# A hybrid encoder layer on one core: small operations sorted and dealt out in the values' stage, and four reorderings around the first loads, the latents and the rotary products

## The chip, the cores and the metric

The kernel runs on one core of one Trainium2 chip. The metric is the time of one execution in device microseconds. The core's engines are TensorE (PE in the profile, with its weight loads as PEld), VectorE (DVE), ScalarE (ACT), GpSimd (POOL) and SyncE (SP, which issues nearly all transfers here). Each works through its own queue of instructions in order and waits on semaphores for the others.

## The reference

One layer with 1024 tokens and 16 meta tokens put in front, model width 1024, all in float32:

```python
def _mixer(u, ...):
    proj = u @ w_in                       # u = rmsnorm(h)
    rq, rk, rv, rg, a_cq, a_ckv, a_kr, a_gret, a_gmla = jnp.split(proj, SPLIT_IDX, axis=-1)
    rq, rk = rope(rq), rope(rk) * RET_DK ** -0.5
    y_ret = head_group_norm(bidir_retention(rq, rk, rv, decay_f, decay_b))
    y_ret = (jax.nn.silu(rg) * y_ret) @ w_ret_out
    q = rmsnorm(a_cq) @ w_uq              # its rotary part is rotated
    k_nope, v = rmsnorm(a_ckv) @ w_uk, rmsnorm(a_ckv) @ w_uv
    k_rope = rope(a_kr)                   # one for all heads
    y_mla = softmax_attention(q, k_nope, k_rope, v) @ w_mla_out
    merged = jax.nn.sigmoid(a_gret) * y_ret + jax.nn.sigmoid(a_gmla) * y_mla
    return merged @ w_o
```

Behind it follow a residual add, an RMSNorm, a SwiGLU feed-forward block, another residual add and a last RMSNorm. The retention needs tables of exponentials of its 16 decay rates (8 heads, two directions).

## The kernel before

**Products.** A float32 operand is split into a rounded high part (a cast on ScalarE) and the rest (a subtraction on VectorE); a product is three matmuls, high by high, high by low, low by high. The helper `split` (line 155) does this for the weights, `bsplit` (278) and `bscale` (284, 285) for the tokens; `split.done` holds the last two instructions. Large products go by Winograd's form of Strassen's scheme: `seven` (lines 184 to 230) loads the four quarters of a weight block (190), forms sums of them (192 to 194, and 210 for the last), splits each of seven operands when it is asked for (212, 213), and issues 12 matmuls of 128 x 512 for each (220). The sums are on GpSimd. The seven partial products are called 11, t2, t3, n1, 21, t4 and 22; `seven_out` (236 to 245) adds them up. Tokens need the same seven combinations, kept in `U`.

**Stages of the first 680 us.** (1) First products: 11 and 21 of seven weight blocks as the tokens arrive, one weight block at a time (`wfirst` splits at 155, products at 344), then the rest of the first two blocks with `rest_out` (305 to 317). The combinations t3 and t4 of the tokens are formed in between, four operations each (412 and 417), with their splits (414, 278, 279). The meta tokens' tile `um` is cleared on GpSimd (406). (2) Two more blocks, the squares of the tokens, and sums of the value weights (545 to 554, GpSimd) that go through device memory. (3) Values: `project_values`, seven products of four steps q each; each step loads a weight (562), splits it and issues twelve matmuls (568), and two for the meta tokens (571) where they belong to the product. Between the products, `between[n]` holds other work: `input_norm` and `decays` behind the second, `decay_rows` (16 exponentials, 513) and a third of the 19 unfinished gates behind the fourth, `decay_columns` and another third behind the fifth, the rest behind the sixth. A gate is loaded, multiplied on VectorE (530), put through silu or sigmoid on ScalarE (531) and stored. `unfinished` lists 16 silus and then 3 sigmoids, and the thirds are taken with a stride of 3. (4) Four rotary blocks of the retention, `project_rope`. (5) The retention of eight heads with blocks of gates and latents as fillers for TensorE. (6) Latents: `project_q`, `project_key`, `project_kv` and the last gate block; `latent_part` (794 to 802) scales, splits and squares a tile and adds the square to `lss`; `latent_norm` sums `lss` over channels with matmuls by ones (161) and makes a norm factor on VectorE and ScalarE. What is left for the meta tokens is put off into `pending` and done within the next block: for the key, a transpose (887), `shared_key` (825 to 832, small operations on 48 x 16 with tables loaded for it), then the norm. (7) The retention's output, four blocks by `seven` (`ret_out`), with the queries' rotary tiles `xx` (`gemm`, lines 139 to 141) made ahead of the third block and rotated (`rotary`, 977 to 984) as that block's results come.

**What sets the order.** The code gives a priority by its order; a planner places every instruction ahead of the run by a simulated clock, first what is ready and earliest in the code, on each engine's queue. `tc.issue_after(ins)` holds the instructions of a block behind `ins` on the same engine. Tiles come from pools; a tile is given out when the one before it in its place is no longer used, and a load into it waits for that.

## Time and profile before

| | |
|---|---|
| median of 3 runs | 1756.33 us (1754.27 to 1756.72) |
| profiled execution | 1753.05 us |
| its span, first to last instruction | 1751.1 us |
| granted TensorE clock, mean | 0.991 |
| TensorE busy | 1698.3 us |
| VectorE busy | 1346.8 us |
| ScalarE busy | 852.2 us |
| GpSimd busy | 763.6 us |

The profile is one execution. The windows view gives, for a stretch in microseconds from the span's start, the busy time and the number of instructions of each engine, the granted TensorE clock (1.00 is full), the mean busy share of the 16 DMA engines and what they moved. The timeline gives instructions in order: start, duration, engine, line, operation, output and inputs, count; in square brackets stands the time in which the engine had been idle before and what ended it. The view by lines gives a group's busy time and the mean of one in ns, and after the bar the idle time before them. A matmul's duration is longer than its distance to the next, since they overlap.

### The profile page before, as it was taken

The page shows a single profiled execution, that of the slowest core. Times are in us where ns is not written, and L with a number is a line of the kernel's source. Part 1 is how long each engine was busy: PE and PEld are TensorE (multiplying, and loading weights), DVE is VectorE, ACT ScalarE, POOL GpSimd, SP SyncE. Part 2 cuts the span into 40 slices and gives each one's busy share as a digit, 9 for nine tenths or more (in the row PEclk, how much of TensorE's full clock was granted, in tenths as well). Part 3 has the DMA queues.
Part 4 walks back from the last instruction along what each step waited for, and adds up shares of the span by engine and source line. Part 5 has one row for each costly group of instructions (what it writes and reads, how often), then busy time and mean ns, then how long its engine had stood idle before and what let it go on. Part 6 is the DMA issues. An engine that isn't in the chain of part 4 may idle for free. (4 is left out here: it accounts for less than half of the span.)

```text
span 1751.1 us, 26268 instructions
## 1 busy us (share of the span) xinstructions
PE 1698.3 (97%) x8644; PEld 1427.5 (82%) x8644; DVE 1346.8 (77%) x2461; ACT 852.2 (49%) x1597; POOL 763.6 (44%) x585
## 2 busy tenths in 40 slices
PE   8999999999999999999999999999999999999998
PEld 6787677888887778999898888788888888788787
DVE  7846778888789876888888768776778887866775
ACT  7426566344424624778787346433333333522335
POOL 2450267575653421324322501566676666523431
PEclk9999999999999999999999999999999999999999
DMA  7876924566546875111122844233344445876612
GB/s 261 290 250 207 296 85 131 164 211 212 193 150 226 254 280 178 30 45 30 30 64 69 272 150 162 80 108 115 129 142 144 139 138 167 273 269 226 231 61 97
DMA packets 169913, 287.15 MB, mean 164 GB/s; under 512 B 20841, under 2 KB 46882, under 8 KB 169778
## 3 DMA queue, kind: packets, MB, share of 16 engines
q1 hardware_dynamic: 168626, 284.44, 48.8%
q8 instruction: 68, 1.11, 0.3%
q10 hardware_dynamic: 1152, 1.05, 0.2%
q14 instruction: 67, 0.55, 0.1%
HBM read 193.28 MB, written 92.06 MB: 163 GB/s over the span
## 5 line engine op out<-in xcount | busy, mean ns | idle before, releaser
L220 PE MATMUL mm<-slot,slot 128*128 128x512 f32 x2604 | 595.0, 390 | 3.6 <-DVE slot L213 1.9
L220 PEld LDWEIGHTS mm<-slot,slot 128*128 128x128 f32 x2604 | 487.3, 188 | 110.2 <-DVE slot L213 4.1
L212 ACT CAST slot<-slot 128x512 fp32r<-128x512 f32 (+1 forms) x385 | 226.8, 596 | 432.2 <-PE mm L220 339.5
L213 DVE TENSOR_TENSOR slot<-slot,slot 128x512 fp32r<-128x512 f32 (+1 forms) x385 | 350.2, 912 | 67.8 <-ACT slot L212 66.9
L192 POOL TENSOR_TENSOR slot<-slot,slot 128x512 f32<-128x512 f32 (+1 forms) x57 | 78.7, 1381 | 329.5 <-DMA slot<-in_w_in 116.5
L220 PE MATMUL mm<-ht,slot 128*128 128x512 f32 x552 | 184.2, 397 | 1.9 <-DVE slot L213 1.9
L220 PE MATMUL mm<-h,slot 128*128 128x512 f32 x440 | 153.2, 408 | 5.8 <-ACT slot L212 2.8
L210 POOL TENSOR_TENSOR slot<-slot,slot 128x512 f32<-128x512 f32 (+1 forms) x57 | 76.5, 1343 | 140.8 <-DVE slot L213 97.6
L155 DVE TENSOR_TENSOR slot<-slot,slot 128x512 fp32r<-128x512 f32 x123 | 97.1, 806 | 40.4 <-ACT slot L155 36.2
L220 PEld LDWEIGHTS mm<-ht,slot 128*128 128x128 f32 x552 | 103.1, 188 | 23.8 <-DVE slot L213 2.7
L155 ACT CAST slot<-slot 128x512 fp32r<-128x512 f32 x123 | 74.5, 618 | 76.7 <-POOL slot L1275 23.4
L1092 DVE TENSOR_SCALAR_CACHE_REDUCE pr<-s,sq_c 128x384 f32<-128x384 f32 (+1 forms) x192 | 103.3, 572 | 7.9 <-PE t L1110 5.3
L220 PE MATMUL mm<-lt,slot 128*128 128x512 f32 x276 | 108.6, 394 | 0.0
L220 PEld LDWEIGHTS mm<-h,slot 128*128 128x128 f32 x440 | 84.2, 193 | 26.3 <-ACT slot L212 5.3
L140 PE MATMUL mm<-slot,slot 128*128 128x512 f32 (+1 forms) x288 | 105.4, 366 | 0.0
L141 PE MATMUL mm<-slot,slot 128*128 128x512 f32 (+1 forms) x288 | 105.3, 366 | 0.0
L139 PE MATMUL mm<-slot,slot 128*128 128x512 f32 (+1 forms) x288 | 105.2, 367 | 0.0
L193 POOL TENSOR_TENSOR slot<-slot,slot 128x512 f32<-128x512 f32 (+1 forms) x57 | 83.4, 1463 | 48.6 <-DVE slot L213 42.3
L1105 DVE TENSOR_TENSOR ptl<-t,pth 128x512 fp32r<-128x512 f32 x128 | 85.7, 684 | 17.7 <-ACT pth L1104 17.2
L1136 POOL TENSOR_TENSOR oa<-oa,ob 64x256 f32<-64x256 f32 x32 | 24.0, 749 | 151.8 <-ACT ob L1135 151.8
L220 PE MATMUL mm<-l,slot 128*128 128x512 f32 x220 | 88.6, 404 | 0.0
L1104 ACT CAST pth<-t 128x512 fp32r<-128x512 f32 x128 | 71.8, 579 | 25.2 <-PE t L1102 24.8
(409 smaller groups left out, 3667.6 us busy)
## 6 DMA issues: line engine op xcount, KB each, us to landing
slot<-in_w_in SPq DMA_DIRECT2D x90, 256.0 KB
f_d<-slot SPq DMA_DIRECT2D x71, 256.0 KB
slot<-f_d SPq DMA_DIRECT2D x71, 256.0 KB
slot<-in_xT SPq DMA_DIRECT2D x48, 256.0 KB
slot<-z_d SPq DMA_DIRECT2D x44, 256.0 KB
slot<-in_w_g SPq DMA_DIRECT2D x44, 256.0 KB
slot<-in_w_u SPq DMA_DIRECT2D x44, 256.0 KB
fl_d<-slot SPq DMA_DIRECT2D x42, 256.0 KB
```

The source lines that it names most:

```text
L139: pe.matmul(ps, sh, mh, start=start, stop=False)
L140: pe.matmul(ps, sh, ml, start=False, stop=False)
L141: pe.matmul(ps, sl, mh, start=False, stop=stop)
L155: split.done = act.copy(hi, t), dve.tensor_sub(lo, t, f(hi))
L192: pool.tensor_add(s1, a21, a22)
L193: pool.tensor_sub(s2, s1, a11)
L210: pool.tensor_sub(s2, s2, a12)
L212: act.copy(hi, side[b])
L213: dve.tensor_sub(low, side[b], f(hi))
L220: pe.matmul(ps, sw[:, ks], sx, start=begins and q == qs[0] and i == 0, stop=q == nq - 1 and i == 2, skip_group_check=True)
L1092: dve.tensor_scalar(pr[:, c], ps[:, :n], sq_c[:, qb : qb + 1], None, ALU.mult, ALU.max, accum_out=mx[:, j : j + 1])
L1105: dve.tensor_sub(pt[1][d], tp, f(pt[0])[d])
```

## The change

There are four groups of edits; no product of the reference is dropped, and nothing is computed in another precision.

First loads and first products: the first token block is issued from ScalarE's queue; the first use of the exponential (with its table load) stands behind the first weight's load; the meta tiles are cleared on VectorE at the start, and 13 matmuls of 384 columns read one of them and write a bank that nobody reads. The first two blocks change places, their weight sums go from GpSimd to VectorE (`adds=dve`), and the token combinations t3 and t4 are made within `rest_out`, behind t2 of both blocks; t4 and 22 are held behind the last weight split.

Values' stage: the work between is listed by product and step (`order`), decays first, then the norm, tables of two heads a step, rows of two heads a step, columns, then one gate a step in nine steps; the other ten gates follow the four rotary blocks, 3, 3, 2 and 2. All of it is held behind the split of its place. Gates are taken in the list's order, silus first.

Latents: both transposes of the kv latents' meta part come before their `latent_part`; the query norm comes before the shared key's meta part, whose transpose is held behind the last of the norm's matmuls.

Rotary products of the queries: the second half of `xx` is made behind 11, t2 and t3 of the third output block, and held behind their last matmul.

```diff
+NIDLE = 13
...
-    act.activation(warm, warm, AF.Exp)
...
     def token_sums(ps, sq, lo, blocks):
...
-            pe.matmul(ps[:n, b : b + 1], sq[:, b * P - lo : b * P - lo + n], ones, start=True, stop=True)
+            norm_sums.append(pe.matmul(ps[:n, b : b + 1], sq[:, b * P - lo : b * P - lo + n], ones, start=True, stop=True))
...
-    def seven(pools, srcs, blocks, meta=None):
+    def seven(pools, srcs, blocks, meta=None, adds=None):
         wr, ws, wh_, wl_, pm_ = pools
+        adds = adds or pool
...
-        pool.tensor_add(s1, a21, a22)
-        pool.tensor_sub(s2, s1, a11)
-        pool.tensor_sub(a21, a21, a11)
+        adds.tensor_add(s1, a21, a22)
+        adds.tensor_sub(s2, s1, a11)
+        adds.tensor_sub(a21, a21, a11)
...
+        for t in (um, umd):
+            dve.memset(f(t), 0.0)
...
             for prod, e, post in group:
                 dve.tensor_add(e, prod("t2"), e)
+            for make in late:
+                make()
...
+            idle = mk(pc, (P, 512), "mm")
+            for i in range(NIDLE):
+                pe.matmul(idle[:, : KT * 48], um.rearrange("p a b -> p (a b)")[:, :P], um.rearrange("p a b -> p (a b)"),
+                          start=True, stop=True)
...
-                x11.append(xload(2 * i, 0))
-                wa11.append(wfirst(win(i)[0], wf if i == 3 else wh1, wf if i == 3 else wl1))
+                x11.append(xload(2 * i, 0, nc.scalar.dma_start if i == 0 else load))
+                raw = wraw(win(i)[0])
+                if i == 0:
+                    act.activation(warm, warm, AF.Exp)
+                wa11.append(split(raw, wf if i == 3 else wh1, wf if i == 3 else wl1))
...
-                pool.memset(f(dst), 0.0)
...
+            def make_t3():
+                with tc.issue_after(made[0].ins), tc.issue_after(made[1].ins):
+                    for q in range(4):
+                        dve.scalar_tensor_tensor(x12[q], x12[q], col(2 * q), x22[q], ALU.mult, ALU.subtract)
+                        U[q]["t3"] = bsplit("t3", x12[q])
+
+            def make_t4():
+                with tc.issue_after(split.done[0].ins), tc.issue_after(split.done[1].ins):
+                    for q in range(4):
+                        dve.scalar_tensor_tensor(x21[q], x21[q], col(2 * q + 1), x11[q], ALU.mult, ALU.subtract)
+                        U[q]["t4"] = bsplit("t4", x21[q])
+                    for q in range(4):
+                        U[q]["22"] = bsplit("22", x22[q])
+
+            rest_out([(seven((wb, wf, wh1, wl1, pc), win(1), U, adds=dve), es[1], rg_post(1)),
+                      (seven(w7, win(0), U, adds=dve), es[0], rg_post(0))], cr, (make_t3, make_t4))
...
-        project_values({1: [input_norm, decays], 3: [decay_rows, lambda: finish_gates(unfinished[0::3])],
-                        4: [decay_columns, lambda: finish_gates(unfinished[1::3])],
-                        5: [lambda: finish_gates(unfinished[2::3])]})
+        order = [("21", 2, decays), ("21", 3, input_norm)]
+        order += [("t2", q, lambda q=q: decay_tables((2 * q, 2 * q + 1))) for q in range(4)]
+        order += [("t3", q, lambda q=q: decay_rows((2 * q, 2 * q + 1))) for q in range(4)]
+        order += [("n1", 0, decay_columns)]
+        order += [(nm, q, lambda: finish(1)) for nm, qs in (("n1", (1, 2, 3)), ("t4", (0, 1, 2)), ("22", (0, 1, 2))) for q in qs]
+        project_values({(nm, q): [f for m, p, f in order if (m, p) == (nm, q)] for nm, q, _ in order})
         for j in range(2):
             project_rope(j, False)
+            with tc.issue_after(split.done[0].ins), tc.issue_after(split.done[1].ins):
+                finish(3 if j == 0 else 2)
             project_rope(j, True)
+            with tc.issue_after(split.done[0].ins), tc.issue_after(split.done[1].ins):
+                finish(3 if j == 0 else 2)
...
                     pe.transpose(pt[:, k * NM : k * NM + NM], t[:, k * P : k * P + P], ident[:NM, :NM])
+                for k in range(2):
                     latent_part(pt[:, k * NM : k * NM + NM], tail, ckv_d[k], column(C_KVN + k), k == 0)
...
                 t = meta_sum(ps, P, 48)
-                pt = mk(pc, (P, 512), "mm")
-                pe.transpose(pt[:48, :NM], t, ident[:NM, :NM])
+                latent_norm(sq_c, 3, 96.0**-0.5, range(NB))
+                with tc.issue_after(norm_sums[-1].ins):
+                    pt = mk(pc, (P, 512), "mm")
+                    pe.transpose(pt[:48, :NM], t, ident[:NM, :NM])
                 ks = work(NM)[:48, :NM]
                 act.copy(ks, pt[:48, :NM])
                 shared_key(ks, tail)
-                latent_norm(sq_c, 3, 96.0**-0.5, range(NB))
...
         for lo, n in RCH:
-            for i in range(2):
-                xx[lo, i] = mk(pc, (P, 512), "mm")
-                gemm(xx[lo, i], wx[i], cq, 3, lo, n)
+            with ExitStack() as behind:
+                if lo:
+                    for b in ("11", "t2", "t3"):
+                        third(b)
+                    behind.enter_context(tc.issue_after(split.mm.ins))
+                for i in range(2):
+                    xx[lo, i] = mk(pc, (P, 512), "mm")
+                    gemm(xx[lo, i], wx[i], cq, 3, lo, n)
```

More of the change, by code (lines that the diff above doesn't have):

```diff
@@ L97, in build @@
     load(cols, A["cols"])
+    warm = mk(cp, (P, 1), "warm")
+    pool.memset(warm, 0.0)
     rstd = mk(cp, (P, NB + 1), "rstd")
@@ L209, in prod @@
                 if b == "22":
-                    pool.tensor_sub(s2, s2, a12)
+                    adds.tensor_sub(s2, s2, a12)
                 hi, low = slot(wh_, F32R)[:, :n], slot(wl_, F32R)[:, :n]
-                act.copy(hi, side[b])
-                dve.tensor_sub(low, side[b], f(hi))
+                split.done = act.copy(hi, side[b]), dve.tensor_sub(low, side[b], f(hi))
                 w[b] = hi, low
@@ L219, in prod @@
                 for i, (sw, sx) in enumerate(((wh, xh), (wh, xl), (wl, xh))):
-                    pe.matmul(ps, sw[:, ks], sx, start=begins and q == qs[0] and i == 0,
-                              stop=q == nq - 1 and i == 2, skip_group_check=True)
+                    split.mm = pe.matmul(ps, sw[:, ks], sx, start=begins and q == qs[0] and i == 0,
+                                         stop=q == nq - 1 and i == 2, skip_group_check=True)
                 if meta and b in meta[1]:
@@ L301, in rg_post, with rest_out @@
             return post
-        def rest_out(group, pl):
+        def rest_out(group, pl, late=None):
+            late = late or ()
             for prod, e, post in group:
                 dve.tensor_add(e, prod("t2"), e)
+            for make in late:
+                make()
             vs = [slot(pl) for _ in group]
@@ L334, in col, with wraw, wfirst @@
                 return column(C_MIX + k)
-            def wfirst(src, ph, plo):
+            def wraw(src):
                 raw = slot(wr1)
                 load(raw, src)
-                return split(raw, ph, plo)
+                return raw
+            def wfirst(src, ph, plo):
+                return split(wraw(src), ph, plo)
             def products(ps, w, b, q, begins):
@@ L495, in decays, with decay_tables @@
             dve.tensor_scalar(dec, dec, -1.0, None, ALU.mult)
+            dts[:] = [slot(xl) for _ in range(2)]
+        def decay_tables(heads):
             ip, im = idx[:, 0:P], idx[:, P : 2 * P]
-            dts = [slot(xl) for _ in range(2)]
-            for h in range(H):
+            for h in heads:
                 lf, lb = dec[:, h : h + 1], dec[:, H + h : H + h + 1]
@@ L504, in decays, with decay_rows @@
                 store(t_d[h], t)
-        def decay_rows():
+        def decay_rows(heads):
             rowf, rowb = idx[:, 2 * P : 3 * P], idx[:, 3 * P : 4 * P]
-            tts = [slot(xl), slot(sr)]
-            for h in range(H):
+            if not tts:
+                tts[:] = slot(xl), slot(sr)
+            for h in heads:
                 hs = slice((h % 2) * 64, (h % 2) * 64 + 64)
@@ L554, in value_weights, with value_product @@
             store(wv_d[3, q], a12)
-        def value_product(nm, meta):
+        def value_product(nm, meta, between):
             banks = [mk(pm, (P, 512), "mm") for _ in range(4)]
@@ L563, in value_product @@
                 hi, lo = split(raw, wh1, wl1)
+                with tc.issue_after(split.done[0].ins), tc.issue_after(split.done[1].ins):
+                    for fn in between.get((nm, q), ()):
+                        fn()
                 xh, xl_ = U[q][nm]
@@ L583, in project_values @@
                 a, meta = (0, M1[nm][1]) if nm in M1 else (1, M2[nm][1]) if nm in M2 else (0, None)
-                banks, mps = value_product(nm, meta)
+                banks, mps = value_product(nm, meta, between)
                 if nm == "t3":
@@ L616, in project_values @@
                     msum[a] = x
-                if n in between:
-                    with tc.issue_after(split.done[0].ins), tc.issue_after(split.done[1].ins):
-                        for fn in between[n]:
-                            fn()
         def project_rope(j, key):
```

32 lines of the change are left out of this document (11 added, 21 removed).

## The prediction

> **What bounds the kernel now.** I read the page's busy shares first, then the busy time of each engine by stage (the windows view, with stages cut where the code changes), then TensorE's waits, then the timeline around each wait.
>
> ```profile
> span 1751.1 us, 26268 instructions
> PE 1698.3 (97%) x8644; PEld 1427.5 (82%) x8644; DVE 1346.8 (77%) x2461; ACT 852.2 (49%) x1597; POOL 763.6 (44%) x585
> ```
>
> TensorE (PE) is busy for 97% of the span, so only 52.8 us are to be had by closing its gaps, beside what it loses at a lower clock. Where they lie:
>
> ```profile
> core 0: us, PE busy (x) PEld busy (x) DVE busy (x) ACT busy (x) POOL busy (x), PEclk, DMA share, GB/s
> ```
> ```profile
> 5.69:52.16 46.47, 41.60 (x162) 32.68 (x163) 42.57 (x58) 33.78 (x59) 9.54 (x6) 0.96 0.72 249
> 52.16:140.00 87.84, 87.84 (x396) 71.82 (x395) 54.93 (x79) 30.86 (x56) 38.59 (x26) 1.00 0.82 276
> 140.00:235.00 95.00, 88.95 (x395) 69.18 (x394) 67.35 (x118) 63.89 (x114) 19.02 (x14) 1.00 0.71 231
> 235.00:300.00 65.00, 62.97 (x304) 49.19 (x303) 54.10 (x71) 44.31 (x74) 46.05 (x29) 1.00 0.29 93
> 300.00:524.00 224.00, 222.40 (x1258) 187.91 (x1257) 184.60 (x445) 82.00 (x143) 139.38 (x96) 1.00 0.57 190
> 524.00:604.00 80.00, 72.64 (x339) 56.85 (x339) 73.11 (x130) 45.00 (x84) 32.51 (x20) 0.91 0.72 230
> 604.00:680.00 76.00, 73.55 (x319) 59.76 (x317) 49.31 (x75) 19.62 (x34) 17.02 (x13) 0.98 0.76 267
> 680.00:1751.10 1071.10, 1048.34 (x5480) 900.08 (x5480) 820.28 (x1491) 530.03 (x1030) 459.99 (x369) 1.00 0.40 132
> ```
>
> Subtract PE busy from the length: the first products idle 4.9 us, the values' stage (140 to 235) 6.1, the rotary products of retention (235 to 300) 2.0, the latents (524 to 604) 7.4, the output product with its rotary part (604 to 680) 2.5. Between 52 and 140 nothing is idle, between 300 and 524 1.6 us. So the edits sit where the gaps are, and dense PE work lies between them: what one place wins is handed on to the next. The clock column matters too; it drops just where PE had waited:
>
> ```profile
> 48.00:52.00 4.00, 4.00 (x12) 3.05 (x12) 4.00 (x8) 1.10 (x2) 0.00 (x0) 0.57 0.75 225
> 552.00:556.00 4.00, 4.00 (x13) 3.42 (x14) 3.78 (x8) 1.72 (x4) 1.01 (x1) 0.50 0.39 138
> ```
> ```profile
> 645.00:649.00 4.00, 3.29 (x8) 2.62 (x9) 4.00 (x6) 1.73 (x4) 2.69 (x2) 0.57 0.78 282
> ```
>
> At a granted 0.57 four busy microseconds do the work of 2.3: 1.7 lost; at 0.50, 2.0; the third window, 3.29 busy, loses 1.4. A wait of two to four microseconds therefore costs its length and about two more.
>
> **The change, part by part.**
>
> *First loads.* The first token block is issued from ScalarE's queue, so the first weight block moves up one place on SP. Thirteen matmuls on a zeroed tile run ahead.
>
> ```profile
> 1.18 0.42 SPq L330 DMA_DIRECT2D slot<-in_xT  x1
> 1.65 0.42 SPq L338 DMA_DIRECT2D slot<-in_w_in  x1
> ```
> ```profile
> 5.69 0.80 PE L344 MATMUL mm<-h,slot 128*128 128x512 f32 x1 [5.69 <-ACT slot L155]
> ```
> ```profile
> 49.29 1.05 PE L344 MATMUL mm<-h,slot 128*128 128x512 f32 x2
> 50.15 0.63 PE L344 MATMUL mm<-l,slot 128*128 128x512 f32 x1
> ```
>
> The second issue moves from 1.65 to 1.18: 0.47 us earlier, and the first real matmul waits for that weight's cast. On ScalarE the exponential's table load now stands behind that issue; it runs while ScalarE waits for data anyway. The idle matmuls cost at a low clock 0.43 us per 512 columns (50.15 less 49.29, over two), so 0.32 for their 384: 13 make 4.2 us.
>
> ```profile
> 1.48 0.42 POOL L406 MEMSET um<- 128x384 f32 x1
> ```
>
> Their operand's memset ends at 1.90 on POOL behind a dozen others; on VectorE, which has nothing ahead of it, it can begin when SP does, near 0.8, so they begin at about 1.2 and at 1.9 at the latest. They end between 5.4 and 6.1, against a first real product possible at about 5.2: they may delay it by 0.2 to 0.9. In return the products behind them start at full clock: bounds 0 (arrival of data sets the pace anyway) to 2.0 (the row at 0.50 above). I take 1.5 for start and clock together, near the middle, since pairs of blocks still have to arrive one after another.
>
> The Trainium skill, "TensorE: Matmul & The Clock Gate", section "What's actually happening", speaks against this edit: the gate looks at a free-running window of about 3.4 us, so how many matmuls stay slow depends on where in the window they fall. By that rule the 13 can end before the gate opens, the term is 0 and the sum stands 1.5 us higher. The low stretch of 48 to 52 agrees with the length, not with the phase, which no row here shows.
>
> *First products.* These rows tell the whole stall:
>
> ```profile
> 35.14 2.72 DVE L412 SCALAR_TENSOR_TENSOR slot<-slot,cols,slot 128x512 f32<-128x512 f32 x4
> ```
> ```profile
> 40.80 5.81 DVE L417 SCALAR_TENSOR_TENSOR slot<-slot,cols,slot 128x512 f32<-128x512 f32 x4
> 46.53 0.68 DVE L155 TENSOR_TENSOR slot<-slot,slot 128x512 fp32r<-128x512 f32 x1
> ```
> ```profile
> 41.41 1.29 POOL L192 TENSOR_TENSOR slot<-slot,slot 128x512 f32<-128x512 f32 x1 [12.35 <-DMA slot<-in_w_in]
> ```
> ```profile
> 47.26 0.73 PE L344 MATMUL mm<-h,slot 128*128 128x512 f32 x2 [4.34 <-DVE slot L155]
> ```
>
> Two groups of four equal operations: 2.72 us with POOL idle, 5.81 while POOL forms weight sums. The weight split that PE needs (L155) stands behind the slow group. The change moves the t3 and t4 blocks behind the split of the second t2 weight, and takes the sums of these two products from POOL to VectorE. Removed: the 4.34 us and the 1.7 at low clock, 6.0. Added on VectorE: 8 sums of 0.68 each, 5.4 us, less the 3.1 us of slowing. VectorE is the next to be late: 42.57 busy of 46.47 here; behind 52 it has 33 us spare in 88. PE has t2 and n1 of both products, 48 matmuls at 87.84/396 = 0.22 us, 10.7 us, to cover t3's blocks (four times 0.68 twice, 5.4) and the four splits (2.7). That suffices, with about a microsecond lost: I take -5.0, bounds -6.0 and 0. The token tiles are freed some microseconds later, so squares and value weights are loaded later; PE needs none of those before 140.
>
> *Values' stage.*
>
> ```profile
> L531 ACT ACT_TABLE_LOAD x7 | 9.0, 1283 | 0.1
> ```
> ```profile
> L513 ACT ACTIVATE slot<-slot,dec 64x128 f32<-64x128 f32 x16 | 5.5, 392 | 0.1
> ```
> ```profile
> 162.79 0.50 PE L568 MATMUL mm<-slot,hn 128*128 128x512 f32 x1 [1.25 <-ACT slot L155]
> ```
> ```profile
> L530 DVE TENSOR_TENSOR slot<-slot,rstd_b 128x512 f32<-128x512 f32 x19 | 14.1, 757 | 7.3 <-DMA slot<-rg_d 5.6 <-DMA slot<-g_d 1.6
> ```
>
> All 16 row exponentials run in one lump of 5.5 us, and the cast that PE needs stands behind it (162.79). Now at most four follow each split, and the 19 gates come one by one, silus before sigmoids: two table loads instead of seven, 5 x 1.283 = 6.4 us less on ScalarE. ScalarE is not the bound (63.89 of 95); what counts is PE's 6.1 us. Some of these waits have other causes (VectorE's tails between products), so -4.0, bounds -6.1 and 0.
>
> Ten gates move on into the retention's rotary products, two or three behind the last split of each.
>
> ```profile
> 204.50 1.39 DVE L530 TENSOR_TENSOR slot<-slot,rstd_b 128x512 f32<-128x512 f32 x1
> ```
>
> A gate's multiplication takes 0.76 in the mean, 1.39 beside POOL, which is busy 46 of 65 us there. VectorE has 65 - 54.1 = 10.9 us spare; ten gates want 7.6 to 13.9. Three of them ahead of the next split are 2.3 to 4.2 us, and the last product of the block before covers 12 x 0.22 = 2.7. So 0 to 1.5 us at each of four places: +2.0, bounds 0 and +6.
>
> *Latents.*
>
> ```profile
> 545.89 1.17 DVE L826 TENSOR_TENSOR small<-small,small 48x16 f32<-48x16 f32 x1 [1.37 <-DMA small<-in_cM]
> ...
> 549.54 1.71 DVE L800 TENSOR_TENSOR lss<-lss,slot 128x512 f32<-128x512 f32 x1
> ```
> ```profile
> 551.30 1.87 PE L161 MATMUL mm<-ones,lss 128*128 128x1 f32 x8 [3.65 <-DVE lss L800]
> ...
> 575.32 0.23 PE L860 MATMUL mm<-ident,sums 16*128 16x16 f32 x1 [0.64 <-DVE small L802]
> ```
>
> VectorE takes the meta tokens' shared key first, waits there for its cosine table, does three tiny operations at 1.2 us, and only then the sum of squares (L800) that PE's token sums wait for. The change puts the norm first and pins the key's transpose behind the token sums: 3.65 and 2.0 of clock go, 5.6. But VectorE is busy 73.11 of 80, so PE arriving earlier meets it again near 575. VectorE itself wins the 1.37 of waiting and up to 3 us of the tiny operations: I take -4.5, bounds -5.6 and -1.4. Issuing the latent transposes together removes the 0.64, but PE's next operand is late too: -0.5, bounds -0.6 and 0.
>
> *Rotary products of the queries.*
>
> ```profile
> 638.79 0.69 DVE L977 TENSOR_TENSOR slot<-mm,slot 128x512 f32<-128x512 f32 x1 [1.25 <-DMA slot<-in_cM]
> ```
> ```profile
> 645.71 0.80 PE L220 MATMUL mm<-h,slot 128*128 128x512 f32 x1 [2.02 <-ACT slot L212]
> ```
>
> All four rotary tiles are now made before the third output product; their VectorE work waits for tables and piles up, and a weight cast waits behind it. Afterwards three of the seven partial products (36 matmuls, 8 us) come between the two halves, so the work of the first half has PE work beside it and the second follows later. Removed 2.02 and 1.4 of clock; I take -3.0, bounds -3.4 and 0.
>
> *Sum.* -1.5 - 5.0 - 4.0 + 2.0 - 4.5 - 0.5 - 3.0 = -16.5 us. The profiled execution took 1753.05 us (1.95 around its span), so 1736.6; the median of the runs shown, 1756.33, lies 3.3 above that execution, and with it the forecast is 1756.33 - 16.5 = 1739.8.
>
> **Rivals.**
>
> *VectorE takes over as the bound.* In the first products it is 92% busy and gets 2.3 us more; in the latents 91%. If t4 and 22, following t3, come late once, and the latents give back all but VectorE's own saving, the first term falls to -1 and the latents to -1.9, and the sum is about -9: 1747. For it: those shares. Against: 33 us of slack right behind the first place.
>
> *The order hardly changes.* The instructions' order is a planner's, and the edits mostly add lower bounds on it; a gap closed at one place may open at another, since the planner did not foresee L800 coming 4 us late. Then the gains and new stalls of 3.65 + 2.0 each cancel, three of them: about 1756. Against: the pins act exactly on the operations that were late.
>
> *The gates hurt the rotary products.* Suppose each batch's loads sit on SP behind a weight load that waits for a buffer:
>
> ```profile
> 117.31 16.48 SPq L562 DMA_DIRECT2D slot<-wv_d  x7
> ```
>
> 2.4 us per issue. VectorE then holds the next split for 4.2 + 2.4, less the 2.7 covered, and 2.0 of clock follow: 5.9 at each of four places, 23.6 instead of the +2.0: 1756.33 - 18.5 + 23.6 = 1761.4. It decides from 18.5/4 = 4.6 us a place. For it: POOL's load there. Against: a DMA share of 0.29, and loads that can be issued early into six buffers.
>
> **How the numbers follow.** About 0.2%, 3.5 us, can be told from no change. Forecast 0.62, VectorE's bound 0.21, order unchanged 0.08, gates 0.09. The first two are faster, 0.83; the third 0.08 the same; the last slower, 0.09. The forecast's own range, with the bounds of its terms partly adding up, is 1730 to 1747; the second rival is taken in and the other two are left out: 1729 to 1751.
>
> **What would show it.** Right: no wait of PE above 1.5 us before 60; clock at 1.00 from 48 to 52; two table loads for the gates; no wait on lss; no wait above 1 us in the third output product. Wrong: waits on the split of weights (L213) between 235 and 300, or in the first products behind t3; a low clock at 550 or 645. The forecast fails as a whole if PE's busy time stays and its idle time falls by less than 5 us.

## The result, and the profile after

| | before | changed | ratio, 95% interval |
|---|---|---|---|
| first chip: median, runs | 1755.30 us (4; 1752.98 to 1756.72) | 1735.49 us (4; 1735.41 to 1735.73) | 0.9892 [0.9878, 0.9905] |
| another chip, the same two kernels | 1756.98 us (11) | 1738.01 us (5; 1734.51 to 1740.04) | 0.9893 [0.9877, 0.9910] |
| profiled execution | 1753.05 us, span 1751.1 | 1735.57 us, span 1733.6 | |

The change makes the kernel 1.1% faster, 19 to 20 us; 16.5 were forecast. The profile after, its span and its busy shares:

```profile
span 1733.6 us, 26277 instructions
PE 1693.8 (98%) x8657; PEld 1425.9 (82%) x8657; DVE 1356.3 (78%) x2471; ACT 839.9 (48%) x1588; POOL 748.5 (43%) x575
```

PE's idle time (span less busy) falls from 52.8 to 39.8 us. The other engines do about what they did, VectorE 9.5 us more (among it the sums it took over). So this is a story of waits, and the waits are read place by place. To do so I count PE's products of 128x512 ("long products" from here on), of which both kernels have 5628 in the same order of stages, and subtract the start times of products with the same number:

| place (number of the last long product) | start after | start before | after less before | won in this stage | forecast |
|---|---|---|---|---|---|
| start and first weights (80) | 26.14 | 26.56 | -0.42 | -0.4 | -1.5 |
| first products, both split blocks (480) | 122.38 | 128.95 | -6.57 | -6.2 | -5.0 |
| values' stage (760) | 194.56 | 208.47 | -13.91 | -7.3 | -4.0 |
| retention's rotary products, start of its heads (1200) | 318.08 | 329.14 | -11.06 | +2.8 | +2.0 |
| heads (1800) | 525.26 | 536.45 | -11.19 | -0.1 | 0 |
| latents (2020) | 596.48 | 608.33 | -11.85 | -0.7 | -5.0 |
| second and third output product (2280) | 655.42 | 671.53 | -16.11 | -4.3 | -3.0 |
| fourth, attention (2360) | 942.99 | 961.57 | -18.58 | -2.5 | 0 |
| to the end | 1733.59 | 1751.10 | -17.51 | +1.1 | 0 |

Stretches of the changed kernel, in the same columns as before (length, busy time and count of PE, weight loads, VectorE, ScalarE, GpSimd; granted clock; DMA share; GB/s):

```profile
48.00:52.00 4.00, 4.00 (x19) 3.32 (x18) 4.00 (x8) 3.37 (x8) 0.00 (x0) 1.00 0.49 145
560.00:564.00 4.00, 1.86 (x5) 1.06 (x6) 3.79 (x9) 1.47 (x4) 2.14 (x1) 0.55 0.95 301
564.00:568.00 4.00, 4.00 (x12) 3.14 (x12) 3.88 (x11) 1.82 (x5) 1.66 (x1) 0.60 0.95 317
592.00:596.00 4.00, 4.00 (x13) 3.18 (x13) 3.91 (x7) 2.18 (x4) 1.02 (x1) 0.68 0.76 243
645.00:649.00 4.00, 4.00 (x19) 3.34 (x18) 3.50 (x6) 1.24 (x3) 0.00 (x0) 1.00 0.99 395
```

The low clock behind the first products and in the third output product is gone, GpSimd no longer works beside VectorE at 48, but in the latents the low clock has only moved, from 552 to 560 and 592 (a granted clock of 0.5 is called half clock below; the windows mix it with full clock at their edges). The timeline of PE there (start, us, line; in brackets the idle time before and what ended it):

```profile
551.32 0.72 PE L223 MATMUL mm<-hn,slot 128*128 128x512 f32 x2 [1.50 <-DVE slot L216]
558.76 1.05 PE L164 MATMUL mm<-ones,lss 128*128 128x1 f32 x8 [0.76 <-DVE lss L837]
561.60 0.79 PE L223 MATMUL mm<-h,slot 128*128 128x512 f32 x1 [1.79 <-ACT slot L216]
...
588.42 0.50 PE L223 MATMUL mm<-ht,slot 128*128 128x512 f32 x1 [1.08 <-ACT ht L283]
...
591.04 1.32 PE L223 MATMUL mm<-h,slot 128*128 128x512 f32 x2 [0.88 <-ACT h L283]
```

The 3.65 us on the key's sum of squares are gone, and PE was 17.4 us ahead at the 1880th product; by the 2020th 5.6 of them had been given back. Those on L283 are for the split of Z, the retention's result, 28 tiles that are loaded, cast and subtracted between 540 and 597.

What the clock took is read from the trace's clock records: PE's busy time at half clock, halved. It is 10.6 us before (from 48, 550, 577, 645 and 874 on) and 4.3 after (from 560 and 591 on). PE's idle time between the first and the last product falls from 40.9 to 32.3. So of the 17.5 us, 8.6 are waits, 6.3 clock, and some 2.5 what is left: products beside a wait take longer, as the values' stage shows below, and the start changed.

### The profile page after: what moved, and what is told of

Same layout as the page of the kernel before. It is cut to its first block, busy times and chain, and to the rows that moved or that the text cites. A ratio compares the mean times of both kernels' runs of the same rounds, so it can differ in the third digit from the quotient of the medians.

```text
span 1733.6 us, 26277 instructions
## 1 busy us (share of the span) xinstructions
PE 1693.8 (98%) x8657; PEld 1425.9 (82%) x8657; DVE 1356.3 (78%) x2471; ACT 839.9 (48%) x1588; POOL 748.5 (43%) x575
## 5 line engine op out<-in xcount | busy, mean ns | idle before, releaser
L216 DVE TENSOR_TENSOR slot<-slot,slot 128x512 fp32r<-128x512 f32 (+1 forms) x385 | 354.3, 924 | 64.3 <-ACT slot L216 63.5
L196 POOL TENSOR_TENSOR slot<-slot,slot 128x512 f32<-128x512 f32 (+1 forms) x55 | 72.9, 1326 | 325.7 <-DMA slot<-in_w_in 86.1
L214 POOL TENSOR_TENSOR slot<-slot,slot 128x512 f32<-128x512 f32 (+1 forms) x55 | 74.1, 1347 | 136.5 <-DVE slot L216 94.4
L156 DVE TENSOR_TENSOR slot<-slot,slot 128x512 fp32r<-128x512 f32 x123 | 101.2, 840 | 40.4 <-ACT slot L156 37.8
L156 ACT CAST slot<-slot 128x512 fp32r<-128x512 f32 x123 | 74.5, 620 | 83.2 <-POOL slot L1320 23.4
L197 POOL TENSOR_TENSOR slot<-slot,slot 128x512 f32<-128x512 f32 (+1 forms) x55 | 81.0, 1472 | 58.4 <-DVE slot L216 55.9
L142 PE MATMUL mm<-slot,slot 128*128 128x512 f32 (+1 forms) x288 | 105.3, 365 | 0.0
L140 PE MATMUL mm<-slot,slot 128*128 128x512 f32 (+1 forms) x288 | 105.2, 367 | 0.0
```

Of the source, the lines that this page charges most:

```text
L140: pe.matmul(ps, sh, mh, start=start, stop=False)
L142: pe.matmul(ps, sl, mh, start=False, stop=stop)
L156: split.done = act.copy(hi, t), dve.tensor_sub(lo, t, f(hi))
L196: adds.tensor_add(s1, a21, a22)
L197: adds.tensor_sub(s2, s1, a11)
L214: adds.tensor_sub(s2, s2, a12)
```

## The experiments

All are edits of the changed kernel, timed against the kernel before on the same chip. Ratios are to that kernel; the changed kernel's is 0.9892 and 0.9893, so a ratio 0.001 higher is 1.75 us more. Where a place is named, the number is the start of that long product less that in the first profile of the changed kernel. Profiles that share the changed start already lie up to 1.55 us apart at the 80th product, so what a stage costs is the difference of two such numbers, at its end and at its start.

**Without the idle products.** `NIDLE = 13` becomes `NIDLE = 0`.

> The changed kernel (1735.5 us) without the 13 idle products ahead of the first real one; all else as changed. Theory (gains are local, and the start of the changed kernel gained only 0.4 us by its 80th long product): the time is 1735.9, up to 1736.5. Rival (the prediction's term: 1.5 us for the clock at the start): 1737.0. A third (the clock window at 48 to 52 belongs to the start as well): 1737.5 or more. What tells: the time of the 80th and of the 160th product of 128x512, beside the changed kernel's.

1739.04 us, ratio 0.9904 [0.9889, 0.9919]: 2 us more by the ratio. Yet the 80th product comes 0.34 us *earlier* than in the first profile, the 1200th 0.14 earlier, the 2340th 0.1 later. Clock is 1.00 from 48 to 52. Idle PE time in all is the same (32.1 against 32.3); what differs is half clock, 7.3 us against 4.3: from 296, 538, 562 and 859 on. Three of these stand behind waits that the changed kernel has as well (1.62 us for 1.18 at 294, and the same two at 561 and 857), one behind a wait of 1.56 at 537 that it has not. So the time is the third expectation's, the place nobody's: the start did not make it. That called for the control.

**The first products: order and engine.** Three kernels: the sums back on GpSimd; the old order too; the old order with the sums on VectorE.

```
- seven(w7, win(0), U, adds=dve)          + seven(w7, win(0), U)                 (GpSimd)
- rest_out([block 1, block 0], cr, (make_t3, make_t4))
+ make_t3(); make_t4(); rest_out([block 0, block 1], cr)                          (old order)
```

> The changed kernel, with the sums of the weights of the two split blocks of the first products put back from VectorE to GpSimd; t3 and t4 are still made late, and block 1 still goes first. Theory (the order of the work gave the gain of the first products, and the engine of the sums is the smaller part): 1737.5, 2 us of the 7 at the 160th product lost. Rival (GpSimd's slow sums, beside VectorE, made the old waits): 1741 to 1742.5, all of it lost. If the engine makes no difference: 1735.5.

> The changed kernel with the order of the first products as it was: t3 and t4 made ahead of the two split blocks, block 0 first, the sums on GpSimd; the idle products and the loads stay as changed. Theory (local gains): the 160th product comes 6.5 to 7 us later than in the changed kernel, and the whole is 1742.0. Rival (what is lost here is taken back in the values' stage, where PE waits for others anyway): 1738 or less.

> The changed kernel with the order of the first products as it was (t3 and t4 ahead of both split blocks, block 0 first), as in the run before with that order, but the sums of the weights stay on VectorE. It is the fourth corner of order and engine: new order and VectorE 0, new order and GpSimd 2 to 3 us later at the 200th long product, old order and GpSimd 12.6 us later (7.4 in the kernel before). Theory (the sums on GpSimd are starved while VectorE has a train of its own: 8.6 us for one sum of 1.3): 3 to 5 us later at the 200th, the price of the order alone. Rival (the order alone is the cause, and the long sum only fills a wait that is there anyway): 7 us or more. Rival (with the sums on VectorE the order costs nothing): within 1 us.

| | ratio | 80th product | 220th | 480th |
|---|---|---|---|---|
| new order, VectorE (changed) | 0.9892 [0.9878, 0.9905] | 0 | 0 | 0 |
| new order, GpSimd | 0.9924 [0.9911, 0.9938] | -1.0 | +1.8 | +1.8 |
| old order, VectorE | 0.9928 [0.9912, 0.9943] | -0.5 | +2.2 | +6.0 |
| old order, GpSimd | 0.9977 [0.9966, 0.9987] | -0.3 | +11.9 | +14.3 |

From the 80th to the 480th product the four take 96.2, 99.1, 102.7 and 110.9 us, and the kernel before took 102.4. So to undo one edit costs 2.8 us (the engine) or 6.5 (the order), to undo both 14.6: they are not additive. Against the kernel before, then, the new order alone wins 3.3 of the 6.2 us and the new engine alone nothing. Of the expectations, the first had its place right (2 us lost) and its rival the total; the second took the loss for half of what it is, and nothing of it is taken back; the third held up to the 200th product (3.5 us), not behind it. The reason why both together cost so much stands on GpSimd and PE in the run with both undone:

```profile
40.97 8.58 POOL L196 TENSOR_TENSOR slot<-slot,slot 128x512 f32<-128x512 f32 x1 [11.70 <-DMA slot<-in_w_in]
49.63 1.26 POOL L197 TENSOR_TENSOR slot<-slot,slot 128x512 f32<-128x512 f32 x1
```
```profile
39.68 2.73 DVE L440 SCALAR_TENSOR_TENSOR slot<-slot,cols,slot 128x512 f32<-128x512 f32 x4
42.33 2.48 DVE L284 TENSOR_TENSOR l<-slot,h 128x512 fp32r<-128x512 f32 x4
44.74 1.28 DVE L156 TENSOR_TENSOR slot<-slot,slot 128x512 fp32r<-128x512 f32 x2
45.94 2.48 DVE L284 TENSOR_TENSOR lt<-slot,ht 128x512 fp32r<-128x512 f32 x4
```
```profile
51.59 0.80 PE L223 MATMUL mm<-ht,slot 128*128 128x512 f32 x1 [8.85 <-ACT slot L216]
```

One sum of 1.3 us took 8.58: it ended 1.1 us after VectorE's train of 14 operations, and those ran at their usual 0.6 to 0.7 each. In the kernel before it was the other way round, GpSimd's three sums at 1.29 to 1.71 and VectorE's four operations at 5.81, not 2.72. If the two shared something by halves, both would lose alike; here the loss falls almost wholly on one of them. The Trainium skill, "SBUF — State Buffer", section "Who interferes with whom", says just this: a VectorE instruction with two SBUF inputs and a GpSimd instruction that reads SBUF contend for a shared pair of ports, and the one that has it blocks the other fully. The trace agrees, and shows more: GpSimd stood still not for one VectorE operation but for the rest of a train. What decides which of the two gets its way the rows do not show, since in both runs GpSimd's sum is recorded 0.04 or 0.05 us ahead of VectorE's next operation (41.41 and 41.46 before, 40.97 and 41.01 here); PE then waits 4.3 us in the one, 8.9 in the other. With the sums on VectorE the old order still costs waits of 1.7 and 1.2 us at 45 and 49, and one at a later block:

```profile
91.90 0.50 PE L223 MATMUL mm<-ht,slot 128*128 128x512 f32 x1 [1.81 <-ACT slot L216]
```

which half clock follows: from the 220th to the 480th product 3.8 us are lost, for a wait of 1.8.

**The values' stage: dealing out and sorting.** The old placement; and the new one with exponentials and silus in turn.

```
- project_values({(nm, q): [...] ...})      + project_values({1: [norm, decays, tables], 3: [rows, 0::3], 4: [columns, 1::3], 5: [2::3]})
- order: all exponentials, then all gates   + order: exponentials and gates in turn
```

> The changed kernel with the exponentials and gates of the values' stage placed as they were: lumps behind products 1, 3, 4 and 5, silus and sigmoids split three ways between them, and all 19 gates inside the stage, none in retention's rotary products. Theory (local gains): the stage takes back its 7.3 us and the rotary products give 2.75, 1740.0. Rival (the prediction's sizes, 4.0 and 2.0): 1737.5. Rival (a later place makes up for it, such as the wait on the retention heads' first loads): 1735.5 to 1736.5.

> The changed kernel with the pieces of work in the values' stage dealt out over as many places, but exponentials and silus in turn, so that about 17 table loads of 1.28 us stand where the changed kernel has 2 or 3. Theory (what gained was the dealing out; a table load ahead of one short piece is hidden, since PE has its next split by then): within 1.5 us of the changed kernel at the end of the stage, 1735.5 to 1737. Rival (the sorting carries the gain: each table load delays a split that PE waits for): the 7.3 us of the stage are lost or more, 1742 to 1752.

The old placement: 1741.33 us, 0.9920 [0.9907, 0.9934]; the stage takes 8.3 us more (-0.96 at the 480th product, +7.35 at the 760th), and the rotary products behind it 2.8 less: 1 us more than the result's 7.3, and its 2.8. In turn: 1737.72, 0.9896 [0.9880, 0.9912]; the stage takes 2.1 us more. PE's waits between 95 and 235 that take longest in all (what waits and for what; total, times, longest), first with the old placement, then in turn:

```profile
PE mm L602 <- ACT slot L156: 3.0, 3, 1.6
```
```profile
PE mm L602 <- DVE slot L629: 0.7, 1, 0.7
PE mm L602 <- DVE slot L631: 0.7, 1, 0.7
```

And the table loads in turn, between 95 and 300 (line, count, busy us, mean ns):

```profile
L557 ACT ACT_TABLE_LOAD x7 | 9.0, 1283 | 0.1
L528 ACT ACT_TABLE_LOAD x3 | 3.8, 1283 | 0.1
L539 ACT ACT_TABLE_LOAD x2 | 2.6, 1283 | 0.0
L501 ACT ACT_TABLE_LOAD x1 | 1.3, 1283 | 0.0
L548 ACT ACT_TABLE_LOAD x1 | 1.3, 1283 | 0.0
```

They are 14, where the changed kernel has 4 (two of them on L557) and the old placement 11: 12.8 us more of ScalarE's time than in the changed kernel, of which PE feels 2.1, and PE never waits on the cast (L156). The theory named the right part, though 2.1 is more than its 1.5. So the dealing out is worth 5 to 6 of the 7.3 us, the sorting about 2.

**The ten late gates.** They go into the values' stage, one or two at each of eleven places; nothing is left among the rotary products.

```
- order += [... finish(1) at nine places]; finish(3 or 2) behind each project_rope
+ order += [finish(2) at eight places, finish(1) at three]
```

> The changed kernel with the ten gates that it runs between retention's rotary products pulled forward into the values' stage: one or two at each of eleven places there, none among the rotary products. The control of the changed kernel gave 1738.0. Theory (the 2.75 us that the rotary stretch gave back are those gates' work on ScalarE ahead of the splits): the stretch from the 900th to the 1200th long product is 2 to 2.75 us shorter, the values' stage under 1 us longer, 1736 to 1737. Rival (two gates at a place delay a split by 1.3 us, and PE waits for it): the stage 2 to 5 us longer, 1738 to 1741. Rival (the stretch waits for the loads behind it in any case): no change, 1738.

1734.68 us, 0.9883 [0.9866, 0.9899]: not told apart from the changed kernel. The stage takes 3.0 us more (-1.6 to +1.4 from the 480th to the 760th product), the rotary products 2.8 less (+1.4 to -1.4). Theory and first rival are both right, each in its stage and neither in its total: the ten gates cost PE about 3 us in either of the two places.

**The key's norm.** `latent_norm` goes back behind `shared_key`, its transpose no longer behind the sums.

> The changed kernel with the key projection's sums behind its transpose and shared key, as they were. Theory (the stall of 3.8 us at 551 comes back, but PE then finds the 28 splits of Z further on, so that the stretch up to 2020 long products loses under 1 us): PE is 4 to 6 us later at the 1880th long product, and 0.7 us later at the 2020th; the whole is 1736 to 1738, one or two charges of the clock of 1.7 us each included. Rival (the prediction's term for the latents): 4.5 us later at the 2020th as well, 1740 or more.

1742.55 us, 0.9918 [0.9904, 0.9931]. The stall returns,

```profile
538.99 1.42 PE L164 MATMUL mm<-ones,lss 128*128 128x1 f32 x8 [3.85 <-DVE lss L837]
```

and with the half clock behind it PE is 5.8 us later at the 1880th product, but only 0.4 at the 2020th (1.5, if the control's profile is taken). These look like the theory's places. But this run stood 1.3 us ahead at the 1800th product, where the latents begin. From there to the 2020th it takes 72.9 us, the changed kernel 71.2 and 69.9 in its two profiles; the ten profiles that leave the latents as changed take 69.7 to 71.8, 70.5 in the mean. So the old order costs 1.7 or 3.0 us in this stage, 2.4 against the mean, and by the 2280th product 3.2: more than the theory's 1, less than the rival's 4.5. The total is the rival's: the median lies 4.5 us above the control's, and from the 1800th product on the two profiles differ by 4.5 as well, of which 1.7 is half clock behind a wait that both have (from 1092 here, none there in the control). What the key's order is worth is thus 2 to 4.5 us, and single profiles do not say it closer.

**The queue of Z's loads.** `load(raw, z_d[...])` becomes `nc.gpsimd.dma_start(raw, z_d[...])`.

> The changed kernel with the 28 loads of Z issued from GpSimd's queue, not SyncE's, where they stand behind stores that wait for ScalarE's sigmoids (up to 2.6 us). Theory (the splits of Z set the pace from 540 to 597, and their loads are held up by what is queued ahead of them): PE's waits of 7.75 us between 551 and 591 shrink by 3 to 6, the 2020th long product is 3 to 6 us earlier, and with one charge of the clock less 1732 to 1735, beside 1738.0 of the control. Rival (the loads are bound by the DMA engines, busy 82% from 540 to 600): under 1 us. Rival (GpSimd's own sums now stand behind loads that wait for a slot): 1 to 4 us slower.

1739.34 us, 0.9902 [0.9885, 0.9919]; the latents (1800th to 2020th product) take 2.3 us more than in the first profile, 3.6 more than in the control. The theory's gain did not come; the time is the second rival's. GpSimd waited as SyncE had (instruction waited for, total, times, longest):

```profile
POOL slot L965 <- DVE lt L284: 8.6, 7, 2.6
POOL slot L214 <- DVE slot L216: 4.8, 3, 2.7
POOL slot L196 <- DMA kr<-in_w_uk: 4.4, 1, 4.4
```

The loads wait for one of four slots, and a slot is free when VectorE's subtraction (L284) has read it; and now they stand behind GpSimd's own sums too. Since this queue has waits of its own, the run does not show whether the loads come late on the other. VectorE's share in this stretch of the changed kernel:

```profile
524.00:600.00 76.00, 68.26 (x310) 52.87 (x309) 68.31 (x104) 39.77 (x78) 31.91 (x20) 0.93 0.79 261
```

68.3 of 76 us busy, and 22.5 of the 23 from 545 to 568, where PE's longest waits lie: that VectorE sets the pace fits; that the stretch would be shorter with less work on it was not tried.

**The queries' rotary products in the old order.** `if lo:` becomes false, all four products first.

> The changed kernel with all four rotary products of the queries ahead of the third output product's block, as they were. Theory: the wait of 2.0 us and the half clock behind it (1.5 us) come back at 640, 3.5 us later at the 2200th long product, and the whole is 1739.0. Rival (the prediction's size): 1738.5. Rival (a later wait takes it back): 1735.5 to 1737.

1735.44 us, 0.9878 [0.9862, 0.9894]: next to nothing is lost (0.4 us from the 2020th to the 2280th product), and nothing is taken back later, since the wait does not come:

```profile
640.00:650.00 10.00, 10.00 (x46) 8.28 (x45) 3.80 (x6) 2.73 (x5) 0.00 (x0) 1.00 0.76 288
```

VectorE was done with the rotary work at 632, in the kernel before with the same text at 650, 18 us later where PE is 14 us later. There it waited 8.5 us for loads between 606 and 652, here 1.3 between 598 and 634; the longest of each (VectorE's timeline, first before, then here):

```profile
632.06 0.69 DVE L944 TENSOR_TENSOR slot<-slot,slot 128x512 f32<-128x512 f32 x1 [3.22 <-DMA slot<-g_d]
```
```profile
621.93 0.69 DVE L1016 TENSOR_TENSOR slot<-mm,slot 128x512 f32<-128x512 f32 x1 [0.79 <-DMA slot<-in_cM]
```

So the order that the change writes out is not what removed the wait. That loads come in time is what the two rows suggest, but it is not shown: in the changed kernel VectorE waits 2.9 us for such a load at 644, and PE does not wait. The other runs narrow it down. From the 2020th to the 2280th product the kernel before takes 63.2 us, the changed kernel 58.9, and each run that undoes one other group (the start, the first products, the values' stage, the gates) 58.9 too, the one with the key's old order 59.8. So no single one of these edits removed the wait; what did stays open.

**The control.** The changed kernel, unaltered.

> The changed kernel itself, unaltered, as a control. Seen so far: every stretch at half clock begins a whole number of 3.413 us after the first clock record of its run, and follows a stretch of that grid in which PE idled 1.3 us or more; the same 1.8 us wait of attention was followed by half clock in three of six kernels. Theory (the grid stands differently in each run, so that a wait is charged or not by where it falls): single runs spread by about 1.7 us or a multiple of it, the median lies between 1735.5 and 1739, and the stretches at half clock in this profile are not all those of the first one (560 and 591). Rival (the grid stands fixed against the program, and the 3.5 us of the kernel without idle products are its own): every run within 0.5 us of 1735.5, and the same two stretches.

1734.51 to 1740.04 us in five runs. The theory holds, with one thing unexplained: the four runs on the first chip lie within 0.3 us of each other. This is the same wait of the same kernel in its two profiles, PE's timeline and the clock behind it, first that of the result, then that of the control:

```profile
857.71 0.39 PE L1176 MATMUL o<-pth,vt 128*128 128x256 f32 x1 [1.81 <-ACT pth L1149]
```
```profile
859.00:863.00 4.00, 4.00 (x33) 3.90 (x33) 2.81 (x10) 3.23 (x8) 1.98 (x2) 1.00 0.08 25
```
```profile
858.37 0.38 PE L1176 MATMUL o<-pth,vt 128*128 128x256 f32 x1 [1.83 <-ACT pth L1149]
```
```profile
859.00:863.00 4.00, 4.00 (x20) 3.74 (x19) 2.37 (x9) 2.02 (x6) 1.15 (x2) 0.57 0.12 35
```

33 products in four microseconds, or 20. Half clock of 3.41 us, 1.7 lost, follows the second and not the first; such a wait is called charged below.

**Five edits together.** The ten gates moved, the rotary order old, five slots for Z, and spare products (their results are overwritten) ahead of two waits:

```
+ if (hh, qc) == (5, 0): 5 x pe.matmul(po, vt[:, 0, 0, :], vt[:, 0, 0:4, :], start=True, stop=True)
+ first norm: 8 x pe.matmul(ps[:, :P], ident, ident, start=True, stop=True)
```

> Five edits of the changed kernel together, each to be read at its own place: the ten gates in the values' stage (as in the run before), the queries' rotary products in the old order (free in its own run), five slots for the loads of Z where there were four, and spare products ahead of two waits that cost half clock in 6 and in 5 of 13 profiles: 5 products of 128x512 (1.1 us) into the bank whose wait at 857 is 1.8 us, and 8 of 128x128 (1.0 us) ahead of the wait of 1.7 us at 1087; their results are overwritten. Theory (a grid stretch of 3.413 us with under 0.8 us of idle PE is never followed by half clock): no half clock behind either place, and the waits there end at the same time as without the products; Z's slots are given back by VectorE's subtractions, so a fifth slot takes 0 to 2 us off the waits from 551 to 591; the whole is 0.986 to 0.988 of the kernel before, about 1731 to 1734. Rival (the idle of PE is not what the grant goes by, or the spare products come too late to cover): half clock behind 857 or 1087 in this profile too, and the ratio stays at 0.988 to 0.989. Rival (spare products lengthen the waits): 1 to 2 us more there, 1736.

1736.31 us, 0.9880 [0.9858, 0.9902]: inside the changed kernel's interval. In attention PE has no gap any more:

```profile
853.38 1.32 PE L1175 MATMUL o<-vt 128*128 128x512 f32 x5
854.53 0.33 PE L140 MATMUL o<-cqh,qh 128*128 128x384 f32 x1
...
856.12 0.28 PE L1178 MATMUL o<-pth,vt 128*128 128x256 f32 x1
```
```profile
853.00:859.00 6.00, 6.00 (x44) 5.74 (x44) 3.59 (x12) 5.54 (x14) 4.12 (x5) 1.00 0.07 18
```

But the spare products do not do it alone. In the changed kernel the product that waits (857.71) has nine products of the next piece of work behind it (L140 to L142); here those nine, 1.6 us from 854.53 on, stand ahead of it (856.12). From the 2340th to the 2360th long product, the spare ones not counted, the stretch takes 261.4 us; in the changed kernel it takes 263.5 when the wait is not charged and 265.3 when it is. How much of this the spare products give and how much the new order was not tried apart.

The others I had put ahead of the wrong norm, and since its results fill two banks there were 16 of them, not 8. The norm with the wait is the second:

```profile
1042.02 1.95 PE L176 MATMUL r<-ident 128*128 128x128 f32 x16
...
1086.05 1.80 PE L180 MATMUL r<-ident,r2c 128*128 128x128 f32 x8 [2.04 <-DVE r2c L1341]
```
```profile
1080.00:1092.00 12.00, 9.96 (x45) 8.20 (x44) 10.57 (x14) 4.73 (x10) 5.96 (x4) 0.86 0.25 66
```

They cost 1.8 us where PE had no wait, and the wait at 1086 was followed by half clock, so the theory of the idle windows was tried in attention alone, where it held. Five slots did not shorten the waits from 550 to 564 (6.5 us, 5.8 in the control); they took away those from 588 to 593, and two others, of 1.2 and 1.1 us, came at 598 and 600. No version is shown to beat the changed kernel.

## Why the prediction was right, and where it was not

The total and its sign were right, 1739.8 forecast and 1735.5 and 1738.0 measured: stages lose and win on their own, dense PE work hands the gain on, and no later stage took much back. That the total fits to within 1 us in the first profile is luck in part: the latents fell 4.3 us short, the values' stage gave 3.3 too much, and the rest (+1.1, -1.2, +0.8, -1.3, and -1.5 where nothing was forecast, in the table's signs) adds 2 us of gain. "VectorE takes over as the bound" came true for the latents alone, "the order hardly changes" and "the gates hurt the rotary products" nowhere.

- *First loads, -1.5.* -0.4 in the first profile, but twelve profiles share this start, and their 80th product lies 0 to 1.55 earlier still, 0.8 in the mean: -1.25 against the one profile of before. The size fits; how far the one profile of before is itself off its mean is not known. How much of it the idle products give: the clock's first record stands at 4.35 to 7.45 us with them, at 9.42 and 10.56 in the two profiles without, which makes about 0.5 us at the 80th product (one profile), within the spread. By the rule of the free window (the Trainium skill, "TensorE: Matmul & The Clock Gate", section "What's actually happening") this term could come out at 0. The runs agree that the moment of full clock shifts, by 3.1 us, less than one step of 3.413; but the 80th product does not follow it (the earliest, 24.59, with 5.65; the next, 24.65, with 7.03). Most of the spread arises within the first ten products, where PE waits 1.21 us for a weight's cast (at 8.76) in the first profile and 0.18 in the earliest.
- *First products, -5.0.* -6.2, past the bound by 0.2. The cause was the one named, and the runs show it to be stronger than its price: with the old order and engine the changed kernel loses 14.6 us here. The new engine alone would have won nothing, the new order alone about half.
- *Values' stage, -4.0.* -7.3, beyond the bound of 6.1. The step that failed is the reading of the gap as length less busy time. In these rows, of the whole stage before and after, PE is busy 97.20 and 95.27 us with the same 433 products:

```profile
105.22:208.47 103.25, 97.20 (x433) 75.60 (x432) 61.49 (x113) 54.89 (x103) 11.27 (x8) 1.00 0.74 241
```
```profile
98.65:194.56 95.91, 95.27 (x433) 76.03 (x432) 58.80 (x105) 41.79 (x88) 17.18 (x12) 1.00 0.75 238
```

  Seven waits fewer, and 1.93 us less busy time: each costs some 0.3 us beside its gap. At the wait of 1.25 us at 162.79, for one, the product ahead of it counts with its full 0.39 us, where the distance to the next is else 0.23, and the first one behind the wait is followed by the next only after 0.34. And of the 6.05 us of gaps 5.4 went, more than the 4 I took. I had named the table loads and the lump in one breath; the lump was 5 to 6 us, the sorting 2.
- *Ten gates among the rotary products, +2.0.* +2.8, in the places named, but only in part by the waits named. These are PE's waits on VectorE's split from 230 to 310, before and after (total, times, longest):

```profile
PE mm L220 <- DVE slot L213: 1.9, 2, 0.9
```
```profile
PE mm L223 <- DVE slot L216: 2.9, 5, 1.2
```

  So 1.1 us are new waits for splits, 0.6 is a longer wait for the heads' first load (1.18 for 0.57), and 1.2 is busy time, 0.3 for each further wait as above.
- *Latents, -4.5 and -0.5.* -0.7 in the first profile, -1.4 against the mean of the ten; the key's order alone 1.7 to 3.0 in this stage, by the run with the old order. This is the term that was taken too large. The stall went as forecast: PE had won 6.2 us in this stage by the 1880th product. The forecast also named why it would not keep them (VectorE is busy 91%, and PE meets it again), but then "VectorE itself wins 1.37 and up to 3" took VectorE's own saving as a gain at the end of the stretch. In its place PE waits 4.6 us between 551 and 564, for weight splits and sums, while VectorE works almost without a pause, and 2.5 us from 588 to 591 for Z, 28 tiles through four slots that the sum did not contain. Which part of VectorE's work ends the stretch stays open: a fifth slot took the waits on Z away, and others came. The forecast's lower bound of 1.4, and the 1.9 of its rival "VectorE takes over as the bound", were the nearer figures.
- *Queries' rotary products, -3.0.* -4.3 for this stage: the wait and the low clock are gone, but not for the reason given, since the old order costs only 0.4 us in the changed kernel. The size is luck; what removed the wait stays open.
- *Not in the forecast:* -2.5 at the start of attention and +1.1 behind it. 1.7 of the first is half clock behind the wait of 1.8 us that both kernels have; in the profile of before it was charged (half clock from 874), in that of after it was not.

Of the signs of being right, all came but one: PE still waits once on lss (558.76), for the next projection's sum. Of the signs of being wrong two came: waits on the split between 235 and 300, of which the kernel before had two as well, and the low clock of 550, which stands at 560 now.

## What to carry to other kernels

Count gains at places, not in one total: the start of the n-th product of a kind in both traces tells in which stage a gain arose and whether a later one kept it. When a stall is removed, ask what chain ends the stretch in which it lies, and take no gain beyond what that chain moves; here a wait in front of dense PE work was gain in full (the values' stage), one in front of a busy VectorE was not (the latents). In this kernel short pieces of a second engine's work, one behind each operation that the first engine waits for, beat lumps by more than sorting them beats switching; and GpSimd's sums beside a train of VectorE's are to be moved or kept apart where PE waits for either.

## What the runs showed of the hardware

**A wait of 1.8 us costs 1.8 or 3.5.** In 14 profiles, the last 30 us left out, 57 stretches of 3.413 us run at half clock, and each lies on a grid of 3.413 us that begins with the run's first clock record (to within 0.001 of a step). 56 of the 57 follow a stretch in which PE idled 0.75 us or more; the one left is the second in a row behind a wait of 3.85. Where PE idled 1.79 or more, half clock always followed; from 0.75 to 1.78 it did or did not. So it matters where the grid cuts a wait. Of the 13 waits at 857 without spare products, the five whose longest piece is 1.77 or more were charged, the five with 1.54 or less were not, and of the three between one was; six in all. The wait of 1.7 at the second norm was charged in five of 13, and there the pieces do not tell which: of ten that the grid leaves whole, four were. The grid stands differently in each run, which fits runs of one kernel that differ by 5.5 us (the control); a comparison of under 3 us needs places, not medians. The Trainium skill, "TensorE: Matmul & The Clock Gate", section "Why this matters for your kernels", warns of gaps of more than about 3 us; the runs say half of that, and the measurement decides.

**A table load costs ScalarE 1.28 us and, ahead of a short piece of work, PE a fraction of it.** Ten more of them, 12.8 us, cost PE 2.1 in the values' stage.
